# Key and query halves in separate stores, and another layout for the inverse's result, in a one-core attention and RWKV step

## The chip, the cores and the metric

The kernel runs on one core of a Trainium2 chip. Its engines are TensorE (PE in the profile; PEld is its weight load), VectorE (DVE), ScalarE (ACT), GpSimd (POOL) and SyncE (SP), which here issues most of the DMAs. Each engine works its instructions off in order, and the engines wait for each other with semaphores. The metric is the device time of one execution in microseconds (us), as the median of several runs.

## What is computed

One layer of a hybrid backbone on 256 context tokens and 1024 latent tokens, width 1024. One input projection feeds two groups, whose gated outputs go through one output projection, a residual and a final norm. Cut to what matters here:

```python
h = rmsnorm(x) * (1 + scale) + shift
u = h @ w_in                       # q, k, v, g_a, u_b, g_b
# A: differential attention, 8 heads, two halves m of 64
q, k = axial_rope(q), axial_rope(k)          # latent tokens only
k_all = concat(cache_k, k); v_all = concat(cache_v, v)
p = softmax(q[m] @ k_all[m] / 8)             # m = 0, 1
o_a = rmsnorm((p[0] - lam * p[1]) @ v_all) * silu(g_a)
# B: RWKV-7, 16 heads of 64, both directions
S = S * w + (S @ -kk) b + v k                # per token
o_b = (norm(S @ r, summed over directions) + bonus) * silu(g_b)
y = rmsnorm(x + gate * (concat(o_a, o_b) @ w_out))
```

The context also gives three outputs: its keys, its values and the final RWKV states.

## The kernel before

**Projection stage.** The 1280 tokens lie normed and transposed in SBUF, each value split into a high and a low part. The weights of `w_in` come in 66 column tiles of 128; each tile is multiplied in three chunks of 512, 512 and 256 tokens, 24 matmuls of 128x128 weights a chunk (`chunk`, L331; the PSUM tile `psg` has four buffers). A plan lists the tiles in order: for each head r, k, v and the gate of group B, and between them the tiles q, k, v and gate of group A. Every tile has a generator that carries its further work; after each chunk all active generators go one step. So the order of instructions on each engine is a mixture made by the plan and by a scheduler that fixes it at build time.

**Group A in that stage** (`b_qk`, L576). A tile `u` (128 rows: two halves `m` of 64 rows `r`; 1280 columns of tokens) is copied from PSUM, stored and read back as `su` with its rows exchanged (L583), turned by the rotary tables on POOL (L589, L590), and added on VectorE (L610). Then ScalarE rounds a chunk of `u` into `hi` (L623), and VectorE leaves the rest `u - hi` in `u` (L624). Both go to DRAM scratch through `spill` (L377), a DMA on SP's queue: `hi` in three stores of 512, 512 and 256 columns, `u` in one of 1280 (640 KB). `hi` has one buffer for heads 0 to 5, so that the next chunk's L623 waits for the store of the one before; the last two heads have a `hi` of full width and store it at once (L618). For `k` the cached 512 keys take the same way first (`ch`, `cv`; L603 to L607; `ch` shares the buffer of `hi`, `cv` lies in the tile `ck`). The destination of all these stores is arranged by L577: scratch `q` is [head, r, part, m, token] and `k` is [head, part, r, m, token], and the store walks them as (m, r, token), while the source is one tile of 128 rows. Counted over the eight heads there are 28 stores for queries and 44 for keys.

**Group B in that stage.** For each pair of heads and direction, and each of five stretches of 256 tokens, VectorE and POOL build `ra` and `bk` (L475 to L484), TensorE makes their products `pg` and the transposes `ptk` (`gram`, L444), VectorE and ScalarE evacuate into `km` (L451, L457; one buffer), and SP stores `km` to `kt` and `bt` and `ra` to `ra` (L459, L461, L478).

**The inverse** (`inverse`, L723). For each block of four head pairs and one stretch of tokens (ten blocks), POOL inverts 128 triangular 32x32 matrices, one in each SBUF lane, in 31 steps of two instructions (L736, L738), between other work. Lane 8g + 4c + x holds the matrix of group g (of 16: four parts f of the stretch, two heads, two directions), chunk c and pair x. The result `tt` goes out with one DMA on POOL's queue (L740) to a DRAM tile `td` laid out [t, lane, s]. `td0` is block 0, written by `b_inv` at the end of the projection stage; later blocks are made by `invert` (L838) during the next stage.

**Recurrence and attention.** `load_early` (L783) loads for each part f the tile `Bt` and, on SP's queue (L791), the tile `Tb` of `td`: 128 rows (four q, 32 t) of 256 values. `prep` (L801) multiplies the two; the recurrence steps use the product. Attention, norms and the output projection fill the time between steps.

Of the kernel before, what the change touches and what calls it, by code (L numbers as in the profile page):

```python
# [10 lines left out]
F32 = mybir.dt.float32  # L11
# [7 lines left out]
P = 128  # L19
# [4 lines left out]
T = TL + TP  # L24
NT = T // P
PAST = 512
# [6 lines left out]
CH = 32  # L33
# [4 lines left out]
HN = 2  # L38
NF = NC // HN
NL = 4  # L40
# [43 lines left out]
def tile_kernel(ctx: ExitStack, tc: tile.TileContext, i: dict, o: dict, heads=H, phases=3):  # L84
    nc = tc.nc

    dram = ctx.enter_context(tc.tile_pool(name="dram", bufs=1, space=DRAM))
    kp = ctx.enter_context(tc.tile_pool(name="kp", bufs=1, reuse_waits="tile"))
    s = {}
# [18 lines left out]
    scratch("y", [heads // NL, T, 2, 2, NL // 2, P])  # L108
    scratch("acc", [T, D])
    gate_d = s["gate"]  # L110
    td0 = dram.tile([CH, P, CH], F32, tag="td0", name="td0")

    ident = kp.tile([P, P], F32, name="ident")
    nc.sync.dma_start(ident, i["ident"])
# [7 lines left out]
    with ExitStack() as p1:  # L122
# [5 lines left out]
        n = 0  # L128
# [4 lines left out]
        n = 128  # L133
# [37 lines left out]
        with ExitStack() as p0:  # L171
# [24 lines left out]
            for n, g in enumerate(WORD):  # L196
                t = sp.tile([P, KD, 256], F32, tag="wa", name=f"wa{g}", bufs=8)
# [143 lines left out]
        def ut(nm):  # L341
            return up.tile([P, UP], F32, tag="u", name=nm)

        def plain(u):
            def f(ps, n0, n):
                nc.scalar.copy(u[:, n0:n0 + n], ps)
            return f
# [28 lines left out]
        def spill(dst, t):  # L376
            nc.sync.dma_start(dst, t)  # L377
# [196 lines left out]
            spill(s[name][j * P:(j + 1) * P, :], g)  # L574

        def b_qk(which, h):  # L576
            dq = lambda v, c: (s["q"][h, :, v, :, c] if which == "q" else s["k"][h, v, :, :, c]).rearrange("r m t -> m r t")  # L577
            off = PAST if which == "k" else 0
            u = ut(f"u{which}{h}")
            yield plain(u)  # L580
            su = ut(f"su{which}{h}")
            for b in range(8):
                nc.sync.dma_start(su[16 * b:16 * b + 16, 0:TL], u[16 * (b ^ 1):16 * (b ^ 1) + 16, 0:TL])  # L583
            if which == "k":
                ck = ap.tile([P, PAST // P, P], F32, tag="w2", name=f"ck{h}")
                nc.sync.dma_start(ck, i["cache_k"][0, 0, :, h].rearrange("(t p) m d -> p t (m d)", p=P))
            yield
            yield
            nc.gpsimd.tensor_tensor(su[:, 0:TL], su[:, 0:TL], sinT, op=ALU.mult)  # L589
            nc.gpsimd.tensor_tensor(u[:, 0:TL], u[:, 0:TL], cosT, op=ALU.mult)  # L590
            if which == "k":
                pk = psm.tile([P, 512], F32, tag="psm", name=f"pk{h}")
                ko = ap.tile([P, 512], F32, tag="hi", name=f"ko{h}", bufs=1)
                for t in range(2):
                    nc.tensor.transpose(pk[:, t * P:(t + 1) * P], u[:, TL + t * P:TL + (t + 1) * P], ident)
                nc.scalar.copy(ko[:, 0:2 * P], pk[:, 0:2 * P])
                nc.sync.dma_start(o["new_k"][0, 0, :, h].rearrange("(t p) m d -> p t (m d)", p=P),
                                  ko[:, 0:2 * P].rearrange("p (t n) -> p t n", n=P))
                pt = psm.tile([P, 512], F32, tag="psm", name=f"pck{h}")
                for t in range(4):  # L600
                    nc.tensor.transpose(pt[:, t * P:(t + 1) * P], ck[:, t, :], ident)
                ch = ap.tile([P, 512], F32, tag="hi", name=f"ch{h}", bufs=1)
                nc.scalar.copy(ch.bitcast(F32R), pt)  # L603
                cv = ck.rearrange("p t n -> p (t n)")
                nc.vector.tensor_tensor(cv.bitcast(F32R), pt, ch, op=ALU.subtract)
                nc.sync.dma_start(dq(0, slice(0, PAST)), ch)
                nc.sync.dma_start(dq(1, slice(0, PAST)), cv)  # L607
            yield
            yield
            nc.vector.tensor_tensor(u[:, 0:TL], u[:, 0:TL], su[:, 0:TL], op=ALU.add)  # L610
            if h >= heads - 2:
                hi = up.tile([P, T], F32, tag="s", name=f"hi{which}{h}", bufs=3)
                for n0, n in CHUNKS:
                    c = slice(n0, n0 + n)
                    nc.scalar.copy(hi[:, c].bitcast(F32R), u[:, c])
                    nc.vector.tensor_tensor(u[:, c].bitcast(F32R), u[:, c], hi[:, c], op=ALU.subtract)
                yield
                spill(dq(0, slice(off, off + T)), hi)  # L618
                spill(dq(1, slice(off, off + T)), u[:, 0:T])
                return  # L620
            for n0, n in CHUNKS:
                hi = ap.tile([P, 512], F32, tag="hi", name=f"hi{which}{h}_{n0}", bufs=1)[:, :n]
                nc.scalar.copy(hi.bitcast(F32R), u[:, n0:n0 + n])  # L623
                nc.vector.tensor_tensor(u[:, n0:n0 + n].bitcast(F32R), u[:, n0:n0 + n], hi, op=ALU.subtract)  # L624
                spill(dq(0, slice(off + n0, off + n0 + n)), hi)
            spill(dq(1, slice(off, off + T)), u[:, 0:T])

        def b_va(h):
            u = ut(f"uv{h}")[:, 0:T]
# [33 lines left out]
        def b_inv():  # L663
            nw = heads * 10
            nc.sync.dma_start(s["wc"][:, 0:nw, :], wcs[:, 0:heads].rearrange("r p i d c -> r (p i d) c"))
            yield
            aw = rp.tile([P, T], F32, tag="td", name="aw0")[:, 0:CH * CH].rearrange("p (t y) -> p t y", y=CH)
            tt = rp.tile([P, T], F32, tag="ta", name="tt0")[:, 0:CH * CH].rearrange("p (t y) -> p t y", y=CH)
            tmp = rp.tile([P, T], F32, tag="kn", name="tmp0")
            for n, _ in enumerate(inverse(nc, s, td0, inv_rows(heads, 0), aw, tt, tmp)):  # L670
                if n % 8 == 0:
                    yield
# [11 lines left out]
        for n, t in enumerate(sr[3:]):  # L684
            m = round((n + 1) * (len(sa) - LAG) / (len(sr) - 3))
# [33 lines left out]
def inv_rows(heads, b):  # L719
    return [(NL * (b // 5) + x, b % 5 - 1) for x in range(NL)]  # L720


def inverse(nc, s, td, rows, aw, tt, tmp):  # L723
    n = 32 * len(rows)
    for x, (p, sg) in enumerate(rows):
        bt = s["bt"][p // NL, sg + 1, :, :, :, :, p % NL].rearrange("f h d t y -> (f h d) t y")
        for c in range(HN):
            nc.sync.dma_start(aw[NL * c + x:n:NL * HN], bt[:, :, c * P + 96:c * P + P])
    yield
    e = nc.gpsimd  # L730
    e.memset(tt[:n], 0.0)
    e.memset(tt.rearrange("p s t -> p (s t)")[:n, 0:CH * CH:CH + 1], 1.0)
    for t in range(CH - 1):
        j, w = t + 1, CH - 1 - t
        mv = tmp[:n, 0:j * w].rearrange("p (w j) -> p w j", w=w)
        e.tensor_tensor(mv, aw[:n, t, t + 1:CH].unsqueeze(2).broadcast_to([n, w, j]),  # L736
                        tt[:n, t:t + 1, 0:j].broadcast_to([n, w, j]), op=ALU.mult)
        e.tensor_tensor(tt[:n, t + 1:CH, 0:j], tt[:n, t + 1:CH, 0:j], mv, op=ALU.add)  # L738
        yield
    nc.gpsimd.dma_start(td[:, 0:n].rearrange("t u s -> u t s"), tt[:n])  # L740


def mix_phase(ctx, tc, i, o, s, ident, nhalf, dram, td0, neglam, subg, lnh, heads, psm):
    nc = tc.nc
# [34 lines left out]
    tds = {0: td0}  # L779
# [3 lines left out]
    def load_early(j):  # L783
        m, f = j // NF, j % NF
        p0, sg = items[m]
        Bt = cp.tile([P, NL, HN, P], F32, tag="Bt", name=f"Bt{j}")
        nc.sync.dma_start(Bt.rearrange("r x c y -> r (x c y)"),
                          s["bt"][p0 // NL, sg + 1, f].rearrange("h d r x y -> (h d r) (x y)"))
        Tb = cp.tile([P, HN, NL, CH], F32, tag="Tb", name=f"Tb{j}")
        src = tds[m].rearrange("t (f q u) s -> f q t (u s)", f=NF, q=4)  # L790
        nc.sync.dma_start(Tb.rearrange("t c x s -> t (c x s)"), src[f])  # L791
        early[j] = (Bt, Tb)

    def prep(j, w, pp, chain):
# [15 lines left out]
    def follow(x, chain):  # L810
        if chain:
            tc.add_manual_dep(x.ins, chain[-1], mybir.DependencyInfo(mybir.DependencyClass.NoSync, mybir.DependencyReason.SCHED_ONLY))
        chain.append(x.ins.name)

    load_early(0)
    for j in range(2):
        load_part(j)
        yield
    for w in duos:
        yield  # L820
        pp = psm.tile([P, 512], F32, tag="psm", name=f"pp{w}")
        prep(0, w, pp, [])
        put(0, w, pp)
    load_early(1)
    yield True

# [11 lines left out]
    def invert(b):  # L838
        rows = inv_rows(heads, b)
        aw = wk.tile([P, CH, CH], F32, tag="aw", name=f"aw{b}")  # L840
        tt = wk.tile([P, CH, CH], F32, tag="tt", name=f"tt{b}")
        tmp = wk.tile([P, CH * CH // 4], F32, tag="tmp", name=f"tmp{b}")
        tds[b] = dram.tile([CH, P, CH], F32, tag=f"td{b % 2}", name=f"td{b}")
        yield from inverse(nc, s, tds[b], rows, aw, tt, tmp)

    bank = [psx.tile([P, 512], F32, name=f"bank{n}") for n in range(2)]
# [60 lines left out]
    def step(j, k, fill):  # L907
# [22 lines left out]
        if k == HN - 1 and j + 1 < n_part:  # L930
            put(j + 1, 1, yb)
            if j + 2 < n_part:
                load_early(j + 2)
# [524 lines left out]
    def inverses():  # L1458
        for b in range(1, n_item):
            yield from invert(b)  # L1460
            yield
# [3 lines left out]
    for t in range(n_tick):  # L1465
        m, c = t // NC, t % NC
        p0, sg = items[m]
        j, k = t // HN, t % HN
# [123 lines left out]
```

## Time and profile before

| | us |
|---|---|
| median of three runs | 2893.0 |
| lowest and highest | 2889.94, 2893.41 |
| the profiled execution | 2881.0 |
| its span | 2878.8 |

| engine | busy us | share of the span |
|---|---|---|
| PE | 2398.6 | 83% |
| PEld | 1931.7 | 67% |
| DVE | 1437.0 | 50% |
| ACT | 1219.6 | 42% |
| POOL | 1132.2 | 39% |

The queues issued from SP carried 427.93 MB in 509024 packets, 59.3% of sixteen DMA engines' span; those issued from POOL 5.75 MB. The shares are averages over stages that work differently, so the views below are read by stage: set-up and first tiles to about 200 us, the projections to 1360, the last attention tiles beside the first inverse to about 1545, then recurrence and attention to 2600, and the end. A wait is given as engine, line, and what released it. In the chain of waits a DMA's piece reaches from its issue to its landing.

### The profile page before, as it was taken

The page shows a single profiled execution, that of the slowest core. Times are in us where ns is not written, and L with a number is a line of the kernel's source. Part 1 is how long each engine was busy: PE and PEld are TensorE (multiplying, and loading weights), DVE is VectorE, ACT ScalarE, POOL GpSimd, SP SyncE. Part 2 cuts the span into 40 slices and gives each one's busy share as a digit, 9 for nine tenths or more (in the row PEclk, how much of TensorE's full clock was granted, in tenths as well). Part 3 has the DMA queues.
Part 4 walks back from the last instruction along what each step waited for, and adds up shares of the span by engine and source line. Part 5 has one row for each costly group of instructions (what it writes and reads, how often), then busy time and mean ns, then how long its engine had stood idle before and what let it go on. Part 6 is the DMA issues. An engine that isn't in the chain of part 4 may idle for free.

```text
span 2878.8 us, 59956 instructions
## 1 busy us (share of the span) xinstructions
PE 2398.6 (83%) x23907; PEld 1931.7 (67%) x23907; DVE 1437.0 (50%) x2794; ACT 1219.6 (42%) x2528; POOL 1132.2 (39%) x1665
## 2 busy tenths in 40 slices
PE   6978789896888987986645779799989899998896
PEld 5866667775776876865533667676768667676674
DVE  5634354543534453542112557566677444445666
ACT  3323233332333332322102667666767555444343
POOL 4233243232233333332623666656765221105364
PEclk9998899997998999998866899899999999799898
DMA  7454545553543544555237978877698987856534
GB/s 234 101 133 103 155 118 133 139 131 97 139 123 101 157 110 125 143 126 123 73 91 185 205 176 191 175 151 174 146 198 223 219 181 183 197 165 198 163 127 164
DMA packets 511399, 437.51 MB, mean 152 GB/s; under 512 B 155063, under 2 KB 449123, under 8 KB 509840
## 3 DMA queue, kind: packets, MB, share of 16 engines
q1 hardware_dynamic: 509024, 427.93, 59.3%
q0 software_dynamic: 2096, 5.75, 1.0%
q8 instruction: 188, 3.08, 0.5%
q14 instruction: 91, 0.75, 0.1%
HBM read 258.69 MB, written 163.86 MB: 147 GB/s over the span
## 4 chain that ended last, share of the span: by engine, by line
PE 42%; DMA 28%; DVE 7%; POOL 6%; SPq 6%; ACT 5%; issue 5%; POOLq 0%; DVEq 0%; ACTq 0%
PE sc L1084 4%; PE po L1129 4%; DMA k<-hik 3%; PE yb L801 3%; PE bank L941 2%; PE pa L1114 2%; DMA wst<-w_out 2%; DMA Tb<-td 2%; DMA bt<-km 2%; DMA acc<-acc 2%; PE pg L450 2%; DMA q<-hiq 2%; DMA k<-ch 2%; PE pso L1337 2%; PE pso L1338 2%
## 5 line engine op out<-in xcount | busy, mean ns | idle before, releaser
L1084 PE MATMUL sc<-ka,q 128*128 128x512 f32 (+1 forms) x832 | 293.2, 446 | 35.9 <-DVE pb L1087 21.9
L1087 DVE TENSOR_SCALAR_CACHE_REDUCE pb<-sc,mn 128x512 f32<-128x512 f32 x256 | 191.4, 748 | 144.2 <-PE sc L1084 136.8
L1129 PE MATMUL po<-vk,aT 128*128 128x128 f32 x1600 | 242.9, 290 | 14.2 <-ACT aT L1116 10.2
L1092 ACT ACTIVATE pb<-pb,mn 128x1536 f32<-128x1536 f32 (+1 forms) x160 | 218.2, 1364 | 80.2 <-DVE pb L1087 78.2
L1129 PEld LDWEIGHTS po<-vk,aT 128*128 128x128 f32 x1600 | 214.4, 198 | 39.2 <-ACT aT L1116 14.4
L482 POOL TENSOR_SCALAR ta<-ta,ka 128x256 f32<-128x256 f32 x80 | 91.5, 1144 | 378.6 <-DVE bk L480 372.9
L457 ACT COPY km<-ptk 64x256 f32<-64x256 f32 x320 | 117.5, 367 | 286.5 <-PE ptk L454 165.3
L736 POOL TENSOR_TENSOR tmp<-aw,tt 128x31 f32<-128x31 f32 (+15 forms) x310 | 165.6, 534 | 102.0 <-DMA aw<-bt 47.5
L450 PE MATMUL pg<-ra,bk 64*64 64x64 f32 x2560 | 101.6, 235 | 113.9 <-POOL bk L484 93.7
L1084 PEld LDWEIGHTS sc<-ka,q 128*128 128x128 f32 x832 | 141.7, 202 | 73.3 <-DVE pb L1087 34.1
L738 POOL TENSOR_TENSOR tt<-tt,tmp 128x31 f32<-128x31 f32 (+15 forms) x310 | 181.1, 584 | 19.3
L450 PEld LDWEIGHTS pg<-ra,bk 64*64 64x64 f32 x2560 | 90.1, 147 | 138.4 <-POOL bk L484 102.5
L451 DVE TENSOR_TENSOR km<-pg,msk 128x512 f32<-128x512 f32 x80 | 55.1, 689 | 243.0 <-PE pg L450 143.2
L807 ACT COPY L<-yb 32x384 f32<-32x384 f32 x312 | 146.6, 470 | 61.4 <-PE yb L801 57.5
L1106 DVE SCALAR_TENSOR_TENSOR pb<-pb,cc,pb 128x512 f32<-128x512 f32 (+1 forms) x208 | 167.0, 850 | 2.0
L1087 DVE TENSOR_SCALAR_CACHE_REDUCE pb<-sc 128x512 f32<-128x512 f32 (+1 forms) x160 | 101.2, 634 | 106.0 <-PE sc L1084 89.4
L1114 PE MATMUL pa<-ident,pb 128*128 128x128 f32 x800 | 139.5, 291 | 16.7 <-DVE acc L1331 9.0
L928 ACT COPY R<-bank 32x256 f32<-32x256 f32 x320 | 116.2, 363 | 67.2 <-PE bank L920 63.2
L1321 POOL TENSOR_TENSOR olo<-of,ohi 128x512 fp32r<-128x512 f32 x30 | 38.4, 1279 | 261.7 <-ACT ohi L1320 214.4
L1116 ACT COPY aT<-pa 128x512 f32<-128x512 f32 (+1 forms) x208 | 115.3, 571 | 60.8 <-PE pa L1114 58.9
L952 DVE TENSOR_TENSOR R<-bank,wc 64x512 f32<-64x512 f32 x156 | 107.0, 686 | 62.4 <-PE bank L941 61.2
L801 PE MATMUL yb<-Bt,Tb 32*32 32x96 f32 x2496 | 108.7, 262 | 31.6 <-DMA Tb<-td 24.3
(354 smaller groups left out, 6489.9 us busy)
## 6 DMA issues: line engine op xcount, KB each, us to landing
acc<-acc SPq DMA_DIRECT2D x50, 512.0 KB
ra<-ra SPq DMA_DIRECT2D x160, 128.0 KB
kt<-km SPq DMA_DIRECT2D x160, 128.0 KB
bt<-km SPq DMA_DIRECT2D x160, 128.0 KB
Bt<-bt SPq DMA_DIRECT2D x40, 512.0 KB
L<-kt SPq DMA_DIRECT2D x40, 512.0 KB
L<-ra SPq DMA_DIRECT2D x40, 512.0 KB
q<-q SPq DMA_DIRECT2D x32, 512.0 KB
```

Of the source, the lines that this page charges most:

```text
L450: nc.tensor.matmul(pg[hs, c, :], bk[hs, c, :], ra[hs, c, :], start=True, stop=True)
L457: nc.scalar.copy(km[64 * h:64 * h + 64, e:NC:2, 0:HD], pt[64 * e:64 * e + 64, :, 64 * h:64 * h + 64])
L736: e.tensor_tensor(mv, aw[:n, t, t + 1:CH].unsqueeze(2).broadcast_to([n, w, j]), tt[:n, t:t + 1, 0:j].broadcast_to([n, w, j]), op=ALU.mult)
L738: e.tensor_tensor(tt[:n, t + 1:CH, 0:j], tt[:n, t + 1:CH, 0:j], mv, op=ALU.add)
L801: follow(nc.tensor.matmul(pp[g, n:n + 96], Tb[g, c, 2 * w + e, :], Bt[g, 2 * w + e, c, 0:96], start=True, stop=True, tile_position=(32 * q ...
L807: nc.scalar.copy(L[96:128, 2 * w:2 * w + 2, q // 2, q % 2, :, 0:96], pp[32 * q:32 * q + 32, 0:192 * HN].rearrange("p (e c y) -> p e c y", ...
L1084: nc.tensor.matmul(sc, q[:, v, m, qc], ka[:, m, 0:kn], start=(v == 0), stop=(v == 1))
L1087: nc.vector.tensor_scalar(pm[:, c * 512:c * 512 + kn], sc, -0.125, mn[:, c - 1:c] if c else None, op0=ALU.mult, op1=ALU.min, accum_out=mn[ ...
L1092: soon.append(lambda: nc.scalar.activation(v, v, AF.Exp, bias=mn[:, c:c + 1], scale=-1.0, accum_out=B["l"][:, m, B["b"]:B["b"] + 1]))
L1106: nc.vector.scalar_tensor_tensor(a, B["p"][1][:, v], B["cc"], a, op0=ALU.mult, op1=ALU.add)
L1114: nc.tensor.transpose(pt[:, t * P:(t + 1) * P], B["p"][0][:, 512 * c + t * P:512 * c + (t + 1) * P], ident)
L1129: nc.tensor.matmul(po, B["aT"][c][:, t * P:(t + 1) * P], vk[:, t, :], start=(c == 0 and t == 0), stop=(c == last and t == nt - 1))
```

## The change

Three things are rewritten; what is computed stays. Each query and key store becomes two, one for each half `m` of 64 rows, both through `spill` on SP's queue; 72 stores become 144. `td` is laid out [group, t, chunk and pair, s] instead of [t, lane, s]. POOL writes it with eight DMAs, one for each of the eight lanes of a group (every eighth lane, 16 lanes each), instead of one. And the load of `Tb` reads four groups, whose 128 rows (q, t) of 256 values now follow one another in DRAM.

```diff
-    td0 = dram.tile([CH, P, CH], F32, tag="td0", name="td0")
+    td0 = dram.tile([4 * NF, CH, NL * HN, CH], F32, tag="td0", name="td0")
...
-            dq = lambda v, c: (s["q"][h, :, v, :, c] if which == "q" else s["k"][h, v, :, :, c]).rearrange("r m t -> m r t")
+            def halves(v, c, t):
+                dst = s["q"][h, :, v, :, c] if which == "q" else s["k"][h, v, :, :, c]
+                for m in range(2):
+                    spill(dst[:, m], t[64 * m:64 * m + 64])
+
...
-                nc.sync.dma_start(dq(0, slice(0, PAST)), ch)
-                nc.sync.dma_start(dq(1, slice(0, PAST)), cv)
+                halves(0, slice(0, PAST), ch)
+                halves(1, slice(0, PAST), cv)
...
-                spill(dq(0, slice(off, off + T)), hi)
-                spill(dq(1, slice(off, off + T)), u[:, 0:T])
+                halves(0, slice(off, off + T), hi)
+                halves(1, slice(off, off + T), u[:, 0:T])
...
-                spill(dq(0, slice(off + n0, off + n0 + n)), hi)
-            spill(dq(1, slice(off, off + T)), u[:, 0:T])
+                halves(0, slice(off + n0, off + n0 + n), hi)
+            halves(1, slice(off, off + T), u[:, 0:T])
...
-    nc.gpsimd.dma_start(td[:, 0:n].rearrange("t u s -> u t s"), tt[:n])
+    for x in range(NL * HN):
+        nc.gpsimd.dma_start(td[:, :, x], tt[x:n:NL * HN])
...
-        src = tds[m].rearrange("t (f q u) s -> f q t (u s)", f=NF, q=4)
-        nc.sync.dma_start(Tb.rearrange("t c x s -> t (c x s)"), src[f])
+        nc.sync.dma_start(Tb.rearrange("t c x s -> t (c x s)"), tds[m][4 * f:4 * f + 4].rearrange("q t u s -> (q t) (u s)"))
...
-        tds[b] = dram.tile([CH, P, CH], F32, tag=f"td{b % 2}", name=f"td{b}")
+        tds[b] = dram.tile([4 * NF, CH, NL * HN, CH], F32, tag=f"td{b % 2}", name=f"td{b}")
```

## The prediction

> **What bounds the kernel now.** I read the table of stages first: one row per stretch, with the length, each engine's busy time (instructions in brackets), then the granted clock, the DMA engines' mean share and GB/s.
>
> ```profile
> 200.00:1360.00 1160.00, 955.97 (x7208) 804.27 (x7207) 513.69 (x813) 362.08 (x700) 362.19 (x401) 0.91 0.49 126
> 1360.00:1545.00 185.00, 106.17 (x629) 89.18 (x627) 33.64 (x67) 26.50 (x54) 72.78 (x89) 0.78 0.40 100
> 1740.00:2600.00 860.00, 803.08 (x11072) 610.50 (x11071) 497.50 (x1116) 537.69 (x1171) 370.91 (x679) 0.94 0.79 183
> ```
>
> From 1740 us TensorE is busy 93% of the time. In the projection stage (200 to 1360) it is busy 956 of 1160 us at clock 0.91, about 870 us of work at full clock: 290 us are lost to idling and to the slow clock that goes with it. In the transition (1360 to 1545) 106 busy us at 0.78 are 83 of 185, so 102 are lost. Two slices of 20 us show that the loss comes in episodes:
>
> ```profile
> 500.00:520.00 20.00, 7.83 (x49) 6.39 (x50) 4.47 (x8) 7.11 (x15) 0.00 (x0) 0.74 0.42 113
> 580.00:600.00 20.00, 20.00 (x193) 17.00 (x191) 10.93 (x20) 8.41 (x13) 4.59 (x6) 1.00 0.46 112
> ```
>
> In the second TensorE never stops. To find what the first waits for, I took the table of waits (engine, line, releaser: total us, times, longest):
>
> ```profile
> POOL ta L482 <- DVE bk L480: 372.9, 69, 29.7
> DVE uk L624 <- ACT hik L623: 127.3, 18, 11.5
> DVE km L451 <- DMA bt<-km: 99.7, 11, 17.9
> ACT hik L623 <- DMA k<-hik: 94.6, 12, 11.6
> PE pg L450 <- POOL bk L484: 93.7, 24, 17.0
> ACT hiq L623 <- DMA q<-hiq: 81.7, 12, 8.9
> PE z L416 <- DVE km L451: 53.4, 6, 12.2
> ACT hik L623 <- DMA k<-ch: 48.9, 6, 10.4
> ```
>
> Backwards: TensorE waits for POOL's `bk`, POOL for VectorE, VectorE (in order) for ScalarE's `hi`, and ScalarE for a key or query store to land, because `hi` has one buffer. The chain of waits (start, us, what) prices the stores and their victims:
>
> ```profile
> by line: DMA k<-hik 7.6%; DMA bt<-km 4.8%; PE pg L450 4.3%; DMA k<-ch 3.5%; DMA k<-uk 3.1%; issue 3.0%; DMA q<-hiq 3.0%; SPq L459 2.8%; PE ptk L454 2.3%; PE psg_v L336 2.0%; PE psg_v L337 2.0%; PE psg_v L335 1.9%; SPq L583 1.7%; DMA w_ada<-
> ...
> 197.51 19.55 DMA w_ada<-w_ada
> ...
> 295.00 11.84 DMA n<-kk
> ...
> 590.72 2.44 DMA ra<-ra
> ...
> 596.07 5.58 DMA vb<-vt
> ...
> 638.28 17.42 DMA q<-uq
> ...
> 818.20 7.88 DMA q<-hiq
> ...
> 840.12 16.90 DMA w_v<-w_in
> ...
> 891.39 2.39 DMA new_k<-ko
> ...
> 922.50 18.77 DMA k<-uk
> ...
> 945.10 2.73 DMA kt<-km
> ```
>
> The first line is the chain between 200 and 1360 alone. A 640 KB store of `uk` takes 18.77 us where one of `vt`, as large, takes 5.58; 256 KB of `hiq` takes 7.88 where 128 KB of `ko` takes 2.39. Why shows where such a store runs alone (904 behind `hik`, 1450 behind `uk`):
>
> ```profile
> 904.00:906.00 2.00, 1.70 (x10) 1.30 (x8) 0.75 (x2) 0.00 (x0) 0.00 (x0) 1.00 0.13 51
> 1450.00:1452.00 2.00, 0.00 (x0) 0.00 (x0) 0.00 (x0) 0.00 (x0) 0.00 (x0) 0.50 0.13 56
> ```
>
> A share of 0.13 is two of sixteen DMA engines, at some 50 GB/s. The two are the two halves `m`, outermost in the destination that line 577 arranges (m r t); `vt` and `ko` have 128 rows outermost. The 24 MB of query and key stores (per head 1280 KB and 1792 KB, eight heads) keep two engines busy for 500 us, and every other transfer that uses all sixteen waits for its share on those two: `n<-kk` moves 5 KB in 11.84 us, right behind a `uk` store.
>
> **Part 1: the stores by 64 rows.** Each half has 64 rows outermost. That such a store spreads over all engines is my reading; the nearest rows are a store of `ra` (64 rows outermost, 128 KB, 2.44 us) and `kt<-km` (32 rows, 128 KB, 2.73 us). The Trainium skill, page "DMA: Bandwidth & Descriptors", section "Why a DMA increments its semaphore by 16 and not by 1", says that a copy runs on the largest number up to 16 that divides the outermost sizes of both sides. By that rule 2 and 128 give two engines and 64 gives sixteen; the trace agrees for the first (0.13).
>
> *Price of a `hi` chunk or cache half:* first half 2.4 to 2.7 us, second issued half a microsecond later, so about 3.2 instead of about 8 (bounds 2.4 and 7.9). *Of a 640 KB store:* 5.58 plus second issue and some company, 7, instead of 17 to 19. On the chain between 200 and 1360: `hik`, `ch`, `hiq` 7.6 + 3.5 + 3.0% of 1160 = 164 us, cut to 40%: -98. `k<-uk` 3.1% and the `uq` piece, 36 + 17 = 53 in three pieces, to 21: -32. Victims: `bt<-km` 4.8% = 56 us; at 2.7 for each of what I take as seven pieces, 19: -37. `w_v` and `w_ada`, 512 KB each, 36 to 18 (9 each, above the 5.58 of the larger `vt`): -18. `n<-kk` to 2.4: -9. Sum -194.
>
> *What it adds:* 72 issues on SP (28 query and 44 key stores become 144), 60 of them in this stretch.
>
> ```profile
> L377 SPq DMA_DIRECT2D q<-hiq x20: 490/532/578, 178.8 to 1457.5; - x20
> L478 SPq DMA_DIRECT2D ra<-ra x160: 574/621/5147, 141.2 to 1347.8; - x160
> L597 SPq DMA_DIRECT2D new_k<-ko x8: 395/400/9684, 254.8 to 1521.9; - x8
> ```
>
> At 0.5 us (between 0.40 and 0.62) that is 30 us of SP; `kt`, `bt`, `ra` and weight loads queue behind it. I charge all of it: +30. The maxima of 5.1 and 9.7 us are issues that themselves stood still, and I count no gain for those. The clock gives back: 956 - 870 = 86 us are lost to it; where TensorE is on the chain (42% of it in the page's fourth part) and most stalls go, -25. Net **-190**. What is late next is the gram loop itself (`bk`, `pg`, `km` with one buffer, its stores); in slices like 580 to 600 it keeps up. The ceiling is 290.
>
> The Trainium skill, page "TensorE: Matmul & The Clock Gate", Part 1, says that an idle window of some 3.4 us halves TensorE's clock and that sustained work restores it. Rows agree (0.50 at 1450, 1.00 at 580); by it stalls of 3 us would cost no clock at all, and this stage could gain up to the 86 us of clock instead of 25, which is the ceiling case below.
>
> **Part 2: the transition.** The last two heads store `hi` whole, and ScalarE's order stands still for buffers that wait for 640 KB stores:
>
> ```profile
> 1412.27 0.59 ACT L346 COPY uk<-psg_ak 128x512 f32<-128x512 f32 x1 [29.95 <-issue]
> 1454.41 0.59 ACT L346 COPY uv<-psg_av 128x512 f32<-128x512 f32 x1 [38.02 <-DMA suk<-uk]
> 1485.31 0.59 ACT L346 COPY uv<-psg_av 128x512 f32<-128x512 f32 x1 [27.02 <-DMA q<-uq]
> 1540.76 0.60 ACT L361 ACTIVATE ga<-psg_ga 128x512 f32<-128x512 f32 x1 [22.08 <-DMA k<-uk]
> ```
>
> That is 117 us of standing. At 7 us a store, 28 stay: -89. But POOL's inverse and rope run here (72.8 busy us) and TensorE needs 83 at full clock. From 185 us, a floor near 85 to 95 with the store of the inverse and first loads in series (about 20): I take 110, **-75** (bounds -30 and -100).
>
> **Part 3: the inverse's result.** One POOL store of 4096 runs of 128 B becomes eight of 512 runs, for ten blocks:
>
> ```profile
> L740 POOL DMA_DIRECT2D td<-tt x10: 1746/1796/1830, 1492.2 to 2185.5; - x10
> L865 POOL DMA_DIRECT2D st<-state_rwkv x8: 604/632/651, 1528.1 to 1533.0; - x8
> POOL tt L731 <- DMA td<-tt: 42.4, 6, 10.6
> ```
>
> A small POOL store takes 0.63, the big one 1.8; in proportion to the runs, 0.63 + 1.17/8 = 0.78, so 6.2 instead of 1.8 a block (bounds 4.8 and 14.4). The first block's is on the path: +4. Nine others, +40 us of POOL, lie in stretches where POOL is busy 371 of 860 and the inverse runs blocks ahead; behind them wait the next `tt` memset (already waiting for the landing) and `olo`. I charge +5, 40 if that cover is gone.
>
> The load `Tb` has four groups `q` outermost before and 128 rows after. Its waits and its longest case:
>
> ```profile
> 1575.87 12.10 DMA Tb<-td
> ...
> PE yb L801 <- DMA Tb<-td: 24.3, 5, 7.4
> ...
> 1576.00:1588.00 12.00, 4.59 (x100) 2.95 (x96) 8.16 (x17) 4.67 (x9) 8.61 (x13) 0.78 1.09 260
> ```
>
> At most 24 us can go. The longest ran while all DMA engines were full (260 GB/s, other loads ahead of it), where spreading helps little: **-10**.
>
> **Sum.** -190 - 75 + 4 + 5 - 10 = -266. The profiled execution is 2881.0 us (span 2878.8 and 2 around it): 2615. The median of the runs shown is 2893.0, 12 above; I add it: 2627, say **2625**.
>
> **Rivals.**
>
> *Another wait takes over.* With the stores fast, the gram loop (VectorE, POOL, TensorE, VectorE, one `km`) is still in order, and POOL's 372.9 us for `bk` is the largest wait. For it: 56 us of the chain is `bt<-km`, which this change touches only through the queue. Against: full slices between stores. If half of -265 is given back, 2760 (2700 to 2840).
>
> *More comes free.* Stalls shorter than TensorE's backlog vanish and the clock stays full: 230 to 250 of 290, 90 in the transition, 20 for `Tb`: about 2540 (2490 to 2560).
>
> *Slower: the halves do not spread.* If two engines is set by something else (the strided destination, say), two half stores last as long as one, and the additions remain: 72 x 0.5 = 36 us of SP and 45 of POOL, about half exposed: 2893 + 40 = 2933 (2905 to 2975). It decides if a lone store still shows 0.13 afterwards. Against it: `vb`, also strided, is three times as fast. The Trainium skill, "DMA: Bandwidth & Descriptors", section "Rules for kernel authors", speaks for this side: two transfers to disjoint partition halves are not worth it, since both spray over the same sixteen engines and serialise, and one of 128 partitions is better. The trace shows the premise missing here: the single transfer has two engines.
>
> *The change does nothing measurable:* gains and additions cancel, 2893.
>
> **Chances.** Forecast 0.62 (2565 to 2700), another wait 0.20, more comes free 0.10, slower 0.05, nothing 0.03. The range takes the forecast's, half of the freer case and most of the second: 2530 to 2770. A measurement of this kernel tells 0.2% (6 us) from no change. Faster 0.92, same 0.03, slower 0.05.
>
> **What would show it.** Right: `q<-hiq` and `k<-hik` land in about 3 us; the waits of L623 fall from 225 us to under 100; no long stretch at share 0.13; the projection stage about 970 us long with TensorE above 90% and its clock above 0.95; the transition about 110 us; POOL's `td` issues about 0.8 us each. Wrong: stores still at 8 us (not spread), or stores fast and `PE pg <- POOL bk` as large as before (another wait), or POOL's eight issues near 1.8 us each and `olo` late behind them.

## The result, and the profile after

The changed kernel takes 2558.9 us (median; 2545.7 to 2561.8) against 2891.5 us for the kernel before on the same chips: a ratio of 0.8856, 95% interval 0.8803 to 0.8909. Its profiled execution took 2561.2 us, with a span of 2559.4, 319.4 less than before. From the page of the changed kernel, the span and the busy time of each engine:

```profile
span 2559.4 us, 60184 instructions
...
PE 2335.7 (91%) x23907; PEld 1887.7 (74%) x23907; DVE 1454.9 (57%) x2794; ACT 1219.4 (48%) x2528; POOL 1167.4 (46%) x1735
```

No engine works much less than it did. TensorE has 63 us less of busy time with the same 23907 matmuls, POOL 35 us more. TensorE's idle time fell from 480 to 224 us, so four fifths of the gain is idling that went. To see where, the two executions have to be cut at the same places in the program, not at the same microseconds. Two places serve, both with one line in either trace (operation, count, duration in ns as min/median/max, then the first and last start in us): the first load of `aw`, which closes the projections, and the first and last product with `Tb`, between which the recurrence runs. Of before:

```profile
L728 SPq DMA_DIRECT2D aw<-bt x80: 513/627/6491, 1357.4 to 2136.6; - x80
...
L801 PE MATMUL yb<-Bt,Tb x2496: 237/241/365, 1549.0 to 2543.4; 32*32 32x96 f32 x192
```

and of the changed kernel:

```profile
L732 SPq DMA_DIRECT2D aw<-bt x80: 519/627/4599, 1135.4 to 1828.7; - x80
...
L805 PE MATMUL yb<-Bt,Tb x2496: 237/241/365, 1248.8 to 2230.8; 32*32 32x96 f32 x192
```

The projections end 222 us earlier, the transition is 192 - 113 = 78 us shorter, the recurrence 994 - 982 = 12 and the end 335 - 329 = 7. The table of stages of the changed kernel, cut at these places (columns as in the prediction: length, busy time of PE, PEld, DVE, ACT and POOL, clock, DMA share, GB/s):

```profile
200.00:1135.00 935.00, 905.82 (x7177) 764.79 (x7176) 521.23 (x810) 362.03 (x695) 362.46 (x400) 0.99 0.61 154
1135.00:1249.00 114.00, 101.88 (x711) 87.13 (x713) 37.47 (x69) 27.77 (x57) 77.78 (x98) 0.96 0.74 171
...
1440.00:2230.00 790.00, 739.84 (x10382) 560.45 (x10381) 466.68 (x1044) 501.80 (x1101) 374.46 (x698) 0.93 0.80 185
```

In the projections TensorE idled 204 us before and idles 29 now; its busy time for nearly the same matmuls fell from 956 to 906 us as the granted clock rose from 0.91 to 0.99. The Trainium skill ("TensorE: Matmul & The Clock Gate", Part 1) says that the clock falls with idle windows and returns with sustained work, and these two rows agree. The waits that the prediction followed backwards (total us, times, longest):

```profile
POOL ta L482 <- DVE bk L480: 293.9, 73, 17.0
...
DVE uk L628 <- ACT hik L627: 34.1, 16, 5.7
...
ACT hiq L627 <- DMA q<-hiq: 26.5, 9, 6.1
...
ACT hik L627 <- DMA k<-hik: 24.5, 10, 5.7
...
PE pg L450 <- POOL bk L484: 20.9, 13, 4.9
DVE km L451 <- DMA bt<-km: 20.9, 4, 7.1
```

Every link shrank: `hik` from 94.6 to 24.5, the wait behind it on VectorE from 127.3 to 34.1, that for `bt<-km` from 99.7 to 20.9, and TensorE's own from 93.7 to 20.9. POOL still waits 294 us for `bk`, as an engine may that is not the bottleneck. The stores themselves, in the view of the tile `hik` (issue on SP's queue, then time to landing) and in a 2 us window in which `k<-hik` and `k<-uk` go out:

```profile
L377 SPq DMA_DIRECT2D k<-hik x40: 445/564/1745, 244.9 to 1204.1; - x40
...
DMA to landing us min/median/max: 1.9/2.4/3.3
```

```profile
776.50:778.50 2.00, 2.00 (x14) 1.70 (x13) 1.45 (x1) 2.00 (x4) 0.00 (x0) 1.00 0.80 168
```

A half lands in 2.4 us at the median, where a whole store took 7.9, and the share is 0.80 where it was 0.13 (small loads share the window).

### The profile page after: what moved, and what is told of

It reads as the page before. It is cut to its first block, busy times and chain, and to the rows that moved or that the text cites. A ratio compares the mean times of both kernels' runs of the same rounds, so it can differ in the third digit from the quotient of the medians.

```text
span 2559.4 us, 60184 instructions
## 1 busy us (share of the span) xinstructions
PE 2335.7 (91%) x23907; PEld 1887.7 (74%) x23907; DVE 1454.9 (57%) x2794; ACT 1219.4 (48%) x2528; POOL 1167.4 (46%) x1735
## 5 line engine op out<-in xcount | busy, mean ns | idle before, releaser
L1088 PE MATMUL sc<-ka,q 128*128 128x512 f32 (+1 forms) x832 | 300.1, 449 | 29.3 <-DVE pb L1091 28.8
L1133 PE MATMUL po<-vk,aT 128*128 128x128 f32 x1600 | 235.2, 287 | 6.0 <-ACT aT L1120 4.3
L482 POOL TENSOR_SCALAR ta<-ta,ka 128x256 f32<-128x256 f32 x80 | 83.1, 1038 | 299.7 <-DVE bk L480 293.9
L1118 PE MATMUL pa<-ident,pb 128*128 128x128 f32 x800 | 134.0, 287 | 17.9 <-DVE acc L1335 10.8
L1118 PEld LDWEIGHTS pa<-ident,pb 128*128 128x128 f32 x800 | 95.6, 144 | 47.2 <-DVE acc L1335 14.5
L945 PEld LDWEIGHTS bank<-R,L 128*64 128x64 f32 x2560 | 94.9, 147 | 39.6 <-issue 16.9
```

The source lines that it names most:

```text
L945: x = nc.tensor.matmul(bank[1][hv(h), o_:o_ + 64], L[:, x_, h, d, k, 0:64], R[:, k, d, x_, hv(h)], start=True, stop=True, tile_position=(0 ...
L1088: nc.tensor.matmul(sc, q[:, v, m, qc], ka[:, m, 0:kn], start=(v == 0), stop=(v == 1))
L1118: nc.tensor.transpose(pt[:, t * P:(t + 1) * P], B["p"][0][:, 512 * c + t * P:512 * c + (t + 1) * P], ident)
L1133: nc.tensor.matmul(po, B["aT"][c][:, t * P:(t + 1) * P], vk[:, t, :], start=(c == 0 and t == 0), stop=(c == last and t == nt - 1))
```

## The experiments

Times are medians; each ratio is to the kernel before, run on the same chip beside it. The stages are those of the profiled execution, cut as above, in us.

| run | median | ratio (95%) | projections | transition | recurrence | end |
|---|---|---|---|---|---|---|
| before | 2891.5 | | 1357.4 | 191.6 | 994.4 | 335.4 |
| change | 2558.9 | 0.8856 (0.8803 to 0.8909) | 1135.4 | 113.4 | 982.0 | 328.6 |
| change again | 2558.2 | 0.8867 (0.8831 to 0.8902) | 1137.7 | 113.4 | 978.3 | 329.1 |
| stores only | 2588.2 | 0.8982 (0.8960 to 0.9004) | 1134.3 | 116.1 | 995.7 | 338.5 |
| inverse only | 2863.0 | 0.9939 (0.9918 to 0.9960) | 1363.0 | 188.8 | 988.1 | 330.4 |
| cut by tokens | 2914.9 | 1.0116 (1.0096 to 1.0135) | 1397.9 | 193.4 | 997.9 | 331.9 |
| quarters | 2548.1 | 0.8851 (0.8832 to 0.8871) | 1144.6 | 112.1 | 963.8 | 325.5 |
| high part only | 2720.1 | 0.9429 (0.9395 to 0.9462) | 1255.0 | 151.2 | 989.6 | 325.9 |
| low part only | 2716.9 | 0.9426 (0.9393 to 0.9459) | 1267.4 | 141.9 | 978.6 | 327.0 |
| one key store | 2559.4 | 0.8868 (0.8839 to 0.8897) | 1130.5 | 113.3 | 982.0 | 328.1 |
| groups outermost | 2560.3 | 0.8877 (0.8843 to 0.8910) | 1137.5 | 114.7 | 980.5 | 325.2 |
| inverse on SP | 2565.1 | 0.8892 (0.8861 to 0.8924) | 1136.0 | 112.9 | 983.8 | 330.6 |
| eight stores, old layout | 2562.0 | 0.8884 (0.8851 to 0.8916) | 1139.5 | 114.0 | 987.3 | 329.0 |
| one store, seven small | 2586.9 | 0.8975 (0.8939 to 0.9012) | 1137.2 | 116.1 | 998.7 | 332.5 |

### Each part alone

*Stores only:* `td`, its one store and its load as before; the rest as in the change.

> The query and key stores by 64 rows alone, the inverse's result as before. Theory (the stores are nearly all of it): 2575 us (2560 to 2590), ratio 0.89; the projection stage ends near 1135 us as with the whole change. Rival (the inverse's layout brings a good part): above 2600 us.

*Inverse only:* the three edits to `td`, and for the query and key stores again one of 128 rows:

```diff
-                for m in range(2):
-                    spill(dst[:, m], t[64 * m:64 * m + 64])
+                spill(dst.rearrange("r m t -> m r t"), t)
```

> The inverse's new layout alone, the stores with two halves outermost as before. Theory: within 15 us of before (2875 to 2900), TensorE's waits for Tb stay near 24 us, POOL's eight issues 0.62 us each. Rival (the inverse's layout brings a good part): 2840 us or less.

The stores alone give 0.8982: some 293 of 2881 us, all of the gain in projections and transition. The inverse alone gives 18 us (0.9939), a little more than the theory allowed, in recurrence and end, and beside the new stores 30 us (2588.2 to 2558.2). That it brings anything measurable needed runs of its own, below.

### Is it the outermost rows, or two smaller stores?

*Cut by tokens:* twice as many stores too, but each walks both halves `m`; inverse as before.

```diff
-                for m in range(2):
-                    spill(dst[:, m], t[64 * m:64 * m + 64])
+                n = (c.stop - c.start) // 2
+                for m in range(2):
+                    cc = slice(c.start + m * n, c.start + m * n + n)
+                    dst = s["q"][h, :, v, :, cc] if which == "q" else s["k"][h, v, :, :, cc]
+                    spill(dst.rearrange("r m t -> m r t"), t[:, m * n:m * n + n])
```

> Two stores for each one of before, as in the change, but cut by tokens: each still walks the two halves m outermost over 128 rows; inverse as before. Theory (the number of outermost rows sets the number of DMA engines): share 0.13 in a lone store, no gain; 72 more issues cost 0 to 40 us: 2890 to 2930. Rival (two smaller stores in flight, whatever their outermost rows): 2650 or less. The layout's rows in DRAM are the same in both, so if the strided destination were the cause, this would change nothing either way.

It is 1.2% slower than before. In its trace a stretch in which SP's last issue was a `k<-hik` store still has the share of two engines (the next loads are issued from 927 us on), and the waits stand where they stood:

```profile
926.00:928.00 2.00, 0.00 (x0) 0.00 (x0) 0.00 (x0) 0.00 (x0) 0.00 (x0) 1.00 0.14 45
```

```profile
PE pg L450 <- POOL bk L484: 100.1, 26, 15.8
...
ACT hiq L629 <- DMA q<-hiq: 84.0, 12, 11.8
...
ACT hik L629 <- DMA k<-hik: 81.6, 12, 10.0
```

This is the prediction's slower rival made real: 72 more issues and no spread, 34 us. But these are not 72 issues of half a microsecond. With two stores behind each other on two engines, the issues on SP stand still themselves, most of all those of the low part (duration in ns as min/median/max):

```profile
L377 SPq DMA_DIRECT2D q<-uq x16: 521/2263/6033, 188.1 to 1506.2; - x16
```

In the changed kernel, which cuts these stores by rows, the sixteen issues take 0.59 us at the median. Added up over the trace, the 144 issues of these stores take 196 us of SP here, the 144 of the changed kernel 88 and the 72 of before 42.

*One key store:* the key scratch with `m` outside `r`, so that both halves are 128 merged rows in DRAM and one store suffices; the loads become two.

```diff
-    scratch("k", [H, 2, HD, 2, NK])
+    scratch("k", [H, 2, 2, HD, NK])
...
+                if which == "k":
+                    spill(s["k"][h, v, :, :, c].rearrange("m r t -> (m r) t"), t)
+                    return
...
-        nc.sync.dma_start(ka, s["k"][h, :, :, :, k0:k0 + n].rearrange("e r m k -> (e r) m k"))
+        for e in range(2):
+            nc.sync.dma_start(ka[64 * e:64 * e + 64], s["k"][h, e, :, :, k0:k0 + n].rearrange("m r k -> r m k"))
```

> The whole change, but the key scratch has m outside r, so that one store of 128 merged rows replaces the two halves of a key (44 stores instead of 88); the key loads become two of 64 rows each (64 instead of 32). If what matters is only the number of outermost rows: as the changed kernel within 10 us, k<-hik lands in 3 us or less. If two halves in flight are better than one store of 128 rows: slower by 15 us or more.

```profile
L377 SPq DMA_DIRECT2D k<-hik x20: 320/344/571, 245.4 to 1198.4; - x20
...
DMA to landing us min/median/max: 2.4/2.4/2.5
```

One store of 128 rows lands in the same 2.4 us as half of it, and the kernel takes as long as the changed one. So halves have no merit of their own; what counts is how many rows stand outermost. The rule of the Trainium skill ("DMA: Bandwidth & Descriptors", section "Rules for kernel authors") that two transfers to disjoint partition halves bring nothing over one agrees with this pair of runs, where both forms have many rows outermost; it did not hold against the store of before, which had two.

### Which of the stores

*High part only* and *low part only*: the stores of `hi` and `ch`, or those of `u` and `cv`, are cut by rows, the others stay as before (`v == 0` or `v == 1` below).

```diff
+                if v == 0:
+                    for m in range(2):
+                        spill(dst[:, m], t[64 * m:64 * m + 64])
+                else:
+                    spill(dst.rearrange("r m t -> m r t"), t)
```

> The whole change, but only the stores of the high part (hi, ch) are cut by rows; the low part (u, cv) is stored with two halves outermost as before, 640 KB on two engines. By the prediction's terms the low part's stores were -32 on the chain of the projections, nearly all of the victims' -72 and most of the transition: 2650 to 2750. Rival (ScalarE's waits for hi are what matters, since hi has one buffer): below 2610.

> The counterpart: only the low part's stores (u, cv) are cut by rows; hi and ch go with two halves outermost. By the prediction's terms hi, ch and their waits were -98 of the projections: 2660 to 2740, the waits of L623's successor still near 200 us. Rival (the 640 KB stores are the trouble, and hi's waits hide beside them): below 2610. If both e5 and this are within 100 us of the change, the two parts share their waits.

2720 and 2717 against 2882 for before: 162 and 165 us. Both hold the inverse's part, worth 18 alone; without it 144 + 147 = 291 us, which is what the stores alone gave (293). So each is worth half, and in the total they add. By stage the sum is looser: in the projections they save 102 and 90 us where the whole change saves 222, in the transition 40 and 50 where it saves 78. They do it in different ways. With only the high part cut, ScalarE's waits for `hi` fall almost to those of the changed kernel, but the victims of the 640 KB stores remain:

```profile
DVE km L451 <- DMA bt<-km: 80.0, 6, 17.2
...
ACT hik L630 <- DMA k<-hik: 32.3, 11, 6.9
...
ACT hiq L630 <- DMA q<-hiq: 27.5, 9, 6.4
```

With only the low part cut, the waits for `hi` stay, and the one for `bt<-km` falls by more than half, though not to the 20.9 us of the changed kernel:

```profile
ACT hiq L630 <- DMA q<-hiq: 84.3, 12, 8.9
...
ACT hik L630 <- DMA k<-hik: 79.5, 12, 8.2
...
DVE km L451 <- DMA bt<-km: 43.8, 8, 9.3
```

### What SP's issues cost

*Quarters:* the whole change, each store cut into two of 32 rows.

```diff
-                for m in range(2):
-                    spill(dst[:, m], t[64 * m:64 * m + 64])
+                for m in range(4):
+                    spill(dst[32 * (m % 2):32 * (m % 2) + 32, m // 2], t[32 * m:32 * m + 32])
```

> The whole change, with each store cut once more, into rows of 32: 288 stores instead of 144. It prices SP's issues. If 72 more issues cost the 30 us that the prediction charged, 144 more cost about 60: 2620. If SP's issues are hidden: 2555 to 2575; q<-hiq still lands in about 3 us.

0.8851 against 0.8867: in the kernel's time, 144 more issues cost nothing that can be measured; it is even a little below the 2555 us expected at the least. They are shorter, 0.42 us at the median instead of 0.56 to 0.59, and add up to 137 us of SP instead of 88. The stages hint at a small price: the projections, where most of these issues lie, took 1144.6 us against 1135.4 and 1137.7 in the two executions of the changed kernel, and 1130.5 with "one key store", which has 44 issues fewer. The recurrence of this run is 14 to 18 us shorter and covers it; why is not known. These are single executions.

### What the inverse's part does

*Change again*, as the measure on one chip:

> The changed kernel again, as the measure for the three beside it: 2545 to 2565 us.

*Groups outermost:* a spare row behind each group in `td`, so that the load of `Tb` has four groups outermost as before; store and load leave the spare row out, nothing else differs, and TensorE, VectorE and ScalarE have the same instructions in the same order.

```diff
-    td0 = dram.tile([4 * NF, CH, NL * HN, CH], F32, tag="td0", name="td0")
+    td0 = dram.tile([4 * NF, CH + 1, NL * HN, CH], F32, tag="td0", name="td0")
...
-        nc.gpsimd.dma_start(td[:, :, x], tt[x:n:NL * HN])
+        nc.gpsimd.dma_start(td[:, 0:CH, x], tt[x:n:NL * HN])
...
-        nc.sync.dma_start(Tb.rearrange("t c x s -> t (c x s)"), tds[m][4 * f:4 * f + 4].rearrange("q t u s -> (q t) (u s)"))
+        nc.sync.dma_start(Tb.rearrange("t c x s -> t (c x s)"), tds[m][4 * f:4 * f + 4, 0:CH].rearrange("q t u s -> q t (u s)"))
```

> The whole change, but the tile td has a spare row of 32x8 values behind each group, so that the load of Tb can't merge groups and rows and walks four groups outermost again; the eight POOL stores stay. If the load's spread brings what the inverse's layout brings (2588 without it, 2559 with it), this is near 2585 us. If the store's new form brings it (POOL no longer waiting for the landing), this stays at 2555 to 2565.

*Eight stores, old layout:* `td`, and the load of `Tb`, as before, but written by eight stores. Again the same order on the three engines. This cut and the next show the inverse's part against the kernel before; the query and key stores are those of the change:

```diff
-    nc.gpsimd.dma_start(td[:, 0:n].rearrange("t u s -> u t s"), tt[:n])
+    for x in range(NL * HN):
+        nc.gpsimd.dma_start(td[:, x:n:NL * HN].rearrange("t u s -> u t s"), tt[x:n:NL * HN])
```

> Query and key stores by 64 rows; the inverse's result in the old layout with the old load, but written by eight POOL stores of 16 lanes. TensorE, VectorE and ScalarE have the changed kernel's instructions in its very order. If the layout (rows that follow one another in DRAM) brings the 29 us between 2588 and 2559: 2580 to 2595. If it is the eight stores, or the order that the scheduler made with them: 2550 to 2565.

*One store, seven small:* the inverse as before, with seven stores of 512 B beside it that nobody reads.

```diff
+    scratch("spare", [8, 16, 8])
...
+    for x in range(NL * HN - 1):
+        nc.gpsimd.dma_start(s["spare"][x], tt[x:n:NL * HN, 0, 0:8])
     nc.gpsimd.dma_start(td[:, 0:n].rearrange("t u s -> u t s"), tt[:n])
```

> Query and key stores by 64 rows; the inverse as before with its one store of 512 KB, and seven stores of 512 B beside it that nobody reads, so that POOL issues eight as in the changed kernel; the scheduler makes a third order of it. If the one large store itself costs the 29 us: 2585 to 2605. If the order decides: anything from 2545 to 2600, and the time from the first recurrence step to the last need not be the 995 us that every kernel with the one store had.

*Inverse on SP:* the eight stores of the change on SP's queue (`nc.sync` for `nc.gpsimd`).

> The whole change with the eight stores of the inverse issued on SP instead of POOL. POOL loses 80 issues of 0.62 us (50 us busy), SP gains 80. If POOL's issues cost something: 2530 to 2550. If they lie beside other work, as predicted: within 8 us of the changed kernel. SP would wait for tt in order, and loads behind it: that could cost up to 20.

The load's spread brings nothing: 2560.3 against 2558.2. Nor does the layout: 2562.0 with the old one. What is left between 2562.0 and 2588.2 is the one store that became eight, and the order of instructions that comes with it. In the four profiled executions with one store the recurrence took 994 to 999 us, in all others 964 to 990; the gap between the groups is smaller than the spread in the second. How eight stores shorten it stays open. It is not POOL's time, as the views of `tt` show: of the stores-only kernel (issue of `td`, then how long POOL stood before the memset of L735),

```profile
L744 POOL DMA_DIRECT2D td<-tt x10: 1746/1796/1830, 1210.6 to 1887.6; - x10
...
  POOL tt L735: 38.8, 7
```

of the changed one,

```profile
L745 POOL DMA_DIRECT2D td<-tt x80: 620/622/747, 1211.7 to 1888.1; - x80
...
  POOL tt L735: 6.8, 2
```

and of the one with the inverse on SP:

```profile
L745 SPq DMA_DIRECT2D td<-tt x80: 513/626/3162, 1212.0 to 1900.2; - x80
...
  POOL tt L735: 53.0, 6
```

Issues and standing together are 18 + 39 = 57, 50 + 7 = 57 and 53 us: POOL loses the same in all three, and the first is slower by 23 us and more. The one with seven small stores beside the large one loses most (70 x 0.48 = 34, and 18 and 36, together 88 us) and takes as long as the first. The scheduler's order is not quite excluded: the kernel with one store and the one with seven small beside it have two different orders, neither that of the changed kernel, and both take 2587 to 2588 us; "quarters", "one key store" and "inverse on SP", with eight, have three more, and take 2548 to 2565. One large store in the changed kernel's very order was not tried.

## Why the prediction was right, point by point

The forecast was 2625 us, -266; the profiled execution gave -319 and the medians -333. The mechanism was right, and the sum too small: 2558.9 us lies in the stated range of 2530 to 2770, but below the forecast's own 2565 to 2700, and within the 2490 to 2560 of the rival "more comes free".

**The two engines** were right. Landing in 2.4 us, the share of 0.80, the pair "cut by tokens" and "one key store" all say that the outermost rows of the destination set the number of engines. The slower rival's price, 40 us forecast and 34 measured when there is no spread, agrees by luck: it counted half of 36 us of SP and 45 of POOL, while "cut by tokens" has no eight POOL stores, and its issues on SP grew by 154 us (42 to 196).

**The projections**, -190 forecast, -222 measured. Three terms were off. The stalls on the chain were put at -194; TensorE's idle time fell by 175. SP's issues were charged with +30, and no gain was counted for issues that stood still; that gain turned out the larger of the two. Added up over the traces, all of SP's issues between 200 us and the first load of `aw` take 538 us before and 451 after, although there are more of them; those longer than 1 us alone fall from 189 us to 56. Of the changed kernel, the two lines whose longest issues were 5.1 and 9.7 us before:

```profile
L478 SPq DMA_DIRECT2D ra<-ra x160: 574/614/2057, 140.7 to 1125.8; - x160
L601 SPq DMA_DIRECT2D new_k<-ko x8: 395/470/1162, 236.3 to 1235.2; - x8
```

The row of `n<-kk`, priced as a slow transfer of 11.84 us, was mostly this too: one of its two issues on SP lasted 8.3 of them. That "quarters" costs so little fits a queue that issues for 451 of 935 us; what covers a later issue was not traced.

The clock was put at -25 and gave -50 (956 to 906 us busy): only the part on the chain was expected back, but with 29 us of idling left in 935 the mean clock is 0.99, so hardly any slow stretch remains. ScalarE's waits before `hi` fell from 225 to 26.5 + 24.5 and 18.0 for `ch`, 69 us; under 100 were forecast.

**The ceiling** of 290 us was too high. It took 870 us of work at full clock as busy time times mean clock, but the mean of 0.91 counts idle microseconds too, and those have a lower clock: in slices of 2 us of the trace before, slices with next to no TensorE work have 0.71 on average, and the clock weighted by TensorE's busy time is 0.945. That makes 904 us of work. After the change it is 906 x 0.99 = 897, so the ceiling was about 263, and 222 of it came. The clock's own loss was about 52 us instead of 86, and 50 of that came back.

**The transition**, -75 forecast, -78 measured: 113 us where 110 was forecast. ScalarE's waits before `uk`, `uv` and `ga` fell from 117 us (the first of the prediction's four lines, 29.95, names no store) to 46, none of which is put down to a store; POOL (78 of 114 us busy) and TensorE (102) fill the stage. That 110 fits so well is in part luck: TensorE's need of 83 us came from the same product with the mean clock and was too low; here it is 102 x 0.96 = 98.

**The inverse**, -1 forecast (+4 and +5 for the store, -10 for the load), -12 and -7 in recurrence and end, 30 us between medians. An issue of 0.78 us was forecast and 0.62 measured. The load's -10 did not exist. What failed is the store's sign: eight issues take 32 us more of POOL, but its standing before the next memset falls by as much, and a gain remains that the trace of before didn't show and that the runs give to the store's number without its cause.

**The rivals.** "Another wait takes over" fell: the gram loop keeps up, and `pg <- bk` shrank with the rest instead of staying. "More comes free" had the clock right and its time is the one that was met, but each of its terms (230 to 250, 90 and 20) lies above what was measured (222, 78 and nothing for the load). "The halves do not spread" fell for halves by rows and is true of halves by tokens. The 12 us that were added for the distance of the median from the profiled execution didn't recur: the changed kernel's profiled execution lies 2 us above its median.

## What to carry to other kernels

When stores are slow, look for a stretch in which one runs alone and read the DMA share: 0.13 is two engines of sixteen, and the cure is an arrangement with many rows outermost (32, 64 and 128 did alike here), by another layout or by more, smaller transfers, whichever is easier. Such a store costs more than its own time: those who wait for it stand (here mostly for the high part's one buffer), and so do other transfers, and issues on the same queue, that come behind it (here mostly behind the low part's 640 KB); the two parts were worth about the same. And for TensorE the slow clock that idle windows bring is a second term of its own: here 50 of 222 us.

## What the runs showed that was not expected

One POOL store of 512 KB in runs of 128 B is 25 us slower over ten blocks than eight of 64 KB to the same places (2588.2 and 2586.9 against 2562.0), though POOL's time doesn't explain it; the cause is open. An issue on POOL takes 0.48 us for 16 runs, 0.62 for 512 and 1.80 for 4096. An issue on SP depends on the form of the transfer: 0.34 us at the median for 128 merged rows, 0.56 for 64 rows of the layout with `m` inside, 0.42 for 32 of them; and `Tb`, 0.43 with merged rows against 0.56 with groups outermost:

```profile
L795 SPq DMA_DIRECT2D Tb<-td x40: 550/563/1104, 1221.1 to 2209.2; - x40
```

That is the kernel with groups outermost; it made no difference to the time. And an issue on SP can stand still for microseconds when stores on two engines are ahead of it: 2.26 us at the median for `q<-uq` when cut by tokens, 0.59 when cut by rows.
